# One layer with an RWKV-7 branch: the inverse's transfers on GpSimd's queue, group 1's k projected first into ar's place, and preparation and group norm in smaller pieces

## The chip, the cores and the metric

The kernel runs on one core of one Trainium2 chip. The metric is device time in microseconds of one execution, given as the median of several runs. The kernel before takes 2217.47 us (three runs, 2214.89 to 2221.9).

## The reference

The program is one layer of a streaming encoder on 256 tokens of width 2048, in fp32: a half-step SwiGLU FFN, two parallel token mixers (latent attention, MLA, and RWKV-7) with gates, a cross-attention into 256 memory tokens, and a second half-step FFN, each between two RMS norms. The change lies in the RWKV-7 mixer, which has 16 heads of width 64:

```python
p = token_shift(proj, mu_shift)              # y + (y_prev - y) * mu
r, k, v, dw, da, dg = jnp.split(p, ...)
w = -jax.nn.softplus(-(w0 + jnp.tanh(dw) @ w_w2)) - 0.5
decay = jnp.exp(-jnp.exp(w))
a = jax.nn.sigmoid(a0 + da @ w_a2)
g = jax.nn.sigmoid(dg) @ w_g2
kk = (k * k_k) per head, divided by its norm
k = k * (1.0 + (a - 1.0) * k_a)
# per token: a_in = -kk, b_in = kk * a
sa = einsum('bhvk,bhk->bhv', state, a_t)
state = state * w_t + sa * b_t + v_t * k_t   # outer products
o_t = einsum('bhvk,bhk->bhv', state, r_t)
# then, per head: o = groupnorm(o) * lnx_w + lnx_b + sum(r * k * r_k) * v
return (o * g) @ w_ob
```

## The kernel before

**Linear layers.** Every weight is loaded in tiles of 128x1024 fp32 (512 KB) by SP into one of four `wraw` buffers, then split by ScalarE (`whi`, a cast, line 319) and VectorE (`wlo`, the remainder, line 320); the halves stand in a ring of three. `lin_tok_steps` (lines 411 to 413) runs three matmuls of 512 columns for each k-step and each of two blocks of 128 tokens; `lin_ch_steps` (lines 375, 379) does the same with the weights stationary. A tile holds the weights for 2.6 us of such matmuls. `self.last_split` and `self.last_cast` name the newest split and cast emitted so far.

**Order of the work.** TensorE's order in the mixer is written by hand: `weave` runs two generators, `rwkv()` (the recurrence) and `fill()` (projections that need no recurrence). Each number that `rwkv()` yields is an amount of filling, in us as the program counts it (0.65 for one token step, 0.66 for one channel step), that goes in before `rwkv()` continues; a function that it yields means filling until that function is true. The other engines follow priorities (the recurrence behind the filling, the splits ahead of all) and the extra dependencies that `after` adds. All transfers of one engine go through that engine's queue in order: SP has the weights, GpSimd (POOL) most small transfers.

**RWKV.** The sixteen heads are two groups (g = 0, 1) of four pairs. `rw_prep` prepares one group: a low-rank matmul for decay and a (line 1038), a cumulative sum on VectorE (1057), the norm of kk (matmul ssp at 1067, a power on GpSimd at 1072, a copy to width 64 at 1077, matmul rnb at 1086), products on VectorE (lines 1088 to 1104), the bonus matmul pb (1110), and four products of 128x1024 with the exponentials, written to `bk` and `ar` (1124 to 1127). k and r of group 0 are projected ahead of the weave; those of group 1 are part of `fill()`, in slots of the tags "k" and "r", of which there is one each, so that group 0's must have been used up. `rw_gram` makes for each pair of chunks of 32 tokens the products of keys with queries, `G` (line 1159). `rw_inverse` inverts 128 triangular 32x32 blocks of it: they go from `G` to DRAM (`ld`, eight transfers), from there into a layout with one block per partition (`LT`), VectorE does 31 steps of two operations (1192, 1195), the result `TT` goes to DRAM (`td`), and `back()` brings it back into `G` in eight transfers (line 1200). Here SP issues all eighteen. `rw_chain` then goes through the eight chunks: po from values (1233) and state (1250), pu with the inverse (1261), the state's update (1277) and the output (1291). Between po of chunk 0 and its pu it yields 62.0, calls `back()` and yields 5.0; the transfers of `back()` are ordered behind the last weight load emitted. `rw_values` loads each chunk's uv on GpSimd's queue, `rw_group_norm` normalises the output of a block of 128 tokens (t = 0 in the chain, t = 1 behind it).

**v.** `rw_proj_v` projects v in two blocks; its tokens are shifted by way of DRAM (`vraw`, `vp`), and the shift's arithmetic is put off by `do_later` until k-step 8 of the next block.

## Time and profile before

| what | value |
|---|---|
| median of three runs | 2217.47 us |
| the profiled execution | 2216.08 us |
| its span (first to last instruction) | 2214.3 us |
| granted TensorE clock, mean | 0.997 |
| TensorE busy | 2181.3 us, 99% |
| VectorE busy | 1467.1 us, 66% |
| ScalarE busy | 1133.5 us, 51% |
| GpSimd busy | 93.2 us, 4% |
| from 880 to 1210 us (the weave): TensorE busy | 322.1 of 330 us |

The profile has a page of totals and several views of the trace: a table by stretches of time, groups of instructions by line, instructions in order of time (with idle time ahead of an instruction in square brackets and what ended it), and the chain of work that ended last. PE is TensorE's matmul, PEld its weight load, DVE VectorE, ACT ScalarE, POOL GpSimd and SP SyncE; a "q" behind an engine's name is its queue. L320 is line 320 of the kernel. Times in the text are microseconds from the start of the span. A matmul's recorded time overlaps the next one's, so that "busy" doesn't mean that no time is lost.

### The profile page before, as it was taken

The numbers are of one execution on the slowest core, as the hardware profiler recorded it, in microseconds if no ns is written. First come the engines' busy times: TensorE is split into PE (matmuls) and PEld (weight loads), VectorE is DVE, ScalarE is ACT, GpSimd is POOL, SyncE is SP. The second block draws the span as 40 slices with busy tenths as digits, with TensorE's granted clock in tenths as the row PEclk, the third lists the DMA queues.
The fourth block names the chain that finished last, engine by engine and source line by source line (L and its number), as shares of the span: only waits on it lengthen the run. The fifth ranks groups of instructions, "written<-read, shape, count | busy, mean of one in ns | idle before, by whom it ended". The sixth has DMA issues, their size and how long they took to land.

```text
span 2214.3 us, 35085 instructions
## 1 busy us (share of the span) xinstructions
PE 2181.3 (99%) x13664; PEld 1944.6 (88%) x13664; DVE 1467.1 (66%) x2164; ACT 1133.5 (51%) x1686; POOL 93.2 (4%) x159
## 2 busy tenths in 40 slices
PE   9999999999999999999999999999999999999997
PEld 8999999988888888888778889988999999998886
DVE  7666666654457677778678766657766666664454
ACT  7555555544446565644444556446555555554442
POOL 0000000000000100100242000000000000000000
PEclk9999999999999999999999999999999999999999
DMA  7666666666666664556767765555666666666664
GB/s 259 222 210 202 202 200 200 201 212 206 209 208 217 207 218 141 168 176 193 245 195 252 266 212 191 172 176 177 199 202 201 202 202 200 200 210 208 209 203 140
DMA packets 138567, 449.31 MB, mean 203 GB/s; under 512 B 24352, under 2 KB 25888, under 8 KB 138144
## 3 DMA queue, kind: packets, MB, share of 16 engines
q1 hardware_dynamic: 131568, 431.94, 60.4%
q0 software_dynamic: 5968, 14.69, 2.1%
q8 instruction: 107, 1.75, 0.3%
q10 hardware_dynamic: 864, 0.44, 0.1%
q14 instruction: 60, 0.49, 0.1%
HBM read 436.51 MB, written 10.49 MB: 202 GB/s over the span
## 4 chain that ended last, share of the span: by engine, by line
PE 86%; DVE 6%; DMA 3%; issue 2%; ACT 2%; POOL 1%; SPq 0%; DVEq 0%; ACTq 0%; POOLq 0%
PE mm L375 31%; PE mm L379 16%; PE mm L411 11%; PE mm L413 11%; PE mm L412 11%; DVE wlo L320 3%; ACT whi L319 1%; DVE X L621 0%; DMA uv<-vsh 0%; DVE tm L1192 0%; DVE TT L1195 0%; PE tr L515 0%; PE xo L1593 0%; DMA ab<-vsh 0%; DMA td<-TT 0%
## 5 line engine op out<-in xcount | busy, mean ns | idle before, releaser
L320 DVE TENSOR_TENSOR wlo<-wraw,whi 128x1024 fp32r<-128x1024 f32 (+3 forms) x792 | 953.5, 1206 | 611.1 <-ACT whi L319 598.9
L319 ACT CAST whi<-wraw 128x1024 fp32r<-128x1024 f32 (+3 forms) x792 | 818.1, 1034 | 789.5 <-PE mm L413 406.8
L375 PE MATMUL mm<-hT,whi 128*128 128x512 f32 x3280 | 1078.0, 383 | 0.6 <-ACT whi L319 0.5
L379 PE MATMUL mm<-hT,wlo 128*128 128x256 f32 x3280 | 881.9, 274 | 1.6 <-DVE wlo L320 1.6
L375 PEld LDWEIGHTS mm<-hT,whi 128*128 128x128 f32 x3280 | 614.4, 190 | 81.6 <-ACT whi L319 1.2
L379 PEld LDWEIGHTS mm<-hT,wlo 128*128 128x128 f32 x3280 | 630.3, 192 | 8.6 <-DVE wlo L320 2.8
L411 PE MATMUL mm<-whi,mh 128*128 128x512 f32 x680 | 257.7, 379 | 0.0
L412 PE MATMUL mm<-wlo,mh 128*128 128x512 f32 x680 | 257.7, 379 | 0.0
L413 PE MATMUL mm<-whi,ml 128*128 128x512 f32 x680 | 257.7, 379 | 0.0
L412 PE MATMUL mm<-wlo,hT 128*128 128x512 f32 (+2 forms) x512 | 180.2, 352 | 5.2 <-DVE wlo L320 5.1
L411 PE MATMUL mm<-whi,hT 128*128 128x512 f32 (+2 forms) x512 | 183.1, 358 | 1.9 <-ACT whi L319 1.7
L413 PE MATMUL mm<-whi,hT 128*128 128x512 f32 (+2 forms) x512 | 179.1, 350 | 0.3 <-DVE hT L506 0.3
L413 PEld LDWEIGHTS mm<-whi,ml 128*128 128x128 f32 x680 | 128.5, 189 | 18.2
L412 PEld LDWEIGHTS mm<-wlo,mh 128*128 128x128 f32 x680 | 128.5, 189 | 18.2
L411 PEld LDWEIGHTS mm<-whi,mh 128*128 128x128 f32 x680 | 128.5, 189 | 18.2
L387 ACT COPY half<-mm 128x256 f32<-128x256 f32 x206 | 75.6, 368 | 120.4 <-PE mm L375 120.4
L412 PEld LDWEIGHTS mm<-wlo,hT 128*128 128x128 f32 x512 | 97.5, 191 | 18.5 <-DVE wlo L320 9.4
L388 DVE TENSOR_TENSOR half<-half,mm 128x256 f32<-128x256 f32 x206 | 86.0, 418 | 40.9 <-ACT half L387 40.9
L411 PEld LDWEIGHTS mm<-whi,hT 128*128 128x128 f32 x512 | 97.5, 190 | 13.8 <-ACT whi L319 2.1
L413 PEld LDWEIGHTS mm<-whi,hT 128*128 128x128 f32 x512 | 97.4, 190 | 10.1 <-DVE hT L506 0.9
L470 POOL TENSOR_TENSOR rstd<-rstd,mhalf 128x1 f32<-128x1 f32 x22 | 14.4, 666 | 1698.2 <-DVE rstd L468 1698.2
L411 PE MATMUL mm<-whi,mT 128*128 128x512 f32 x128 | 48.7, 380 | 0.0
(305 smaller groups left out, 1752.0 us busy)
## 6 DMA issues: line engine op xcount, KB each, us to landing
wraw<-in_w_ffn_up SPq DMA_DIRECT2D x171, 512.0 KB, 3.7
wraw<-in_w_ffn_gate SPq DMA_DIRECT2D x170, 512.0 KB, 3.6
wraw<-in_w_ffn_down SPq DMA_DIRECT2D x168, 512.0 KB, 4.2
wraw<-in_w_in SPq DMA_DIRECT2D x124, 512.0 KB, 4.1
wraw<-in_w_o SPq DMA_DIRECT2D x32, 512.0 KB, 4.0
wraw<-in_w_ckv SPq DMA_DIRECT2D x32, 512.0 KB, 3.9
wraw<-in_w_oa SPq DMA_DIRECT2D x16, 512.0 KB, 3.6
wraw<-in_w_ob SPq DMA_DIRECT2D x16, 512.0 KB, 4.6
```

Of the source, the lines that this page charges most:

```text
L319: cast = self.last_cast = nc.scalar.copy(out=hi[:, e], in_=raw[:, e])
L320: self.last_split = nc.vector.tensor_sub(out=lo[:, e], in0=raw[:, e], in1=hi[:, e].bitcast(F32))
L375: both = lambda: nc.tensor.matmul(ps[j], hi[:, s], self.woven(x[:, k]), start=(k == 0), stop=(k == nk - 1))
L379: nc.tensor.matmul(ps[j][:, 0, :], lo[:, s], self.woven(x[:, k, 0]), start=False, stop=False)
L387: nc.scalar.copy(out=tokens, in_=low)
L388: nc.vector.tensor_add(tokens, tokens, high)
L411: nc.tensor.matmul(ps[t], part(xh, t, k), hi, start=(k == first), stop=False)
L412: nc.tensor.matmul(ps[t], part(xh, t, k), lo, start=False, stop=False)
L413: self.last_mm = nc.tensor.matmul(ps[t], part(xl, t, k), hi, start=False, stop=(k == last))
L470: nc.gpsimd.tensor_tensor(out=r, in0=r, in1=self.mhalf, op=ALU.pow)
```

## The change

Five things are changed. **The inverse's eighteen transfers** are issued by GpSimd instead of SP, the way back included, which now stands at the end of `rw_inverse`; `back`, the yield of 5.0 behind it and `last_fetch` are gone. **Group 1's k** is projected first, into the first half of `ar`'s part for group 1 (which is written only at the end of that group's preparation); then comes one block of `out_a`, then r, then the other three blocks of `out_a`. Before, two blocks of `out_a` came first, then k, r and the last two blocks. **Preparation:** kf, the factor of ta and the factor r_k on r go from VectorE to ScalarE; the remaining products on VectorE each stand behind the last split emitted so far (`behind`), with yields of 2.6 us between them, and so do the four products into `bk` and `ar`. **Group norm** for t = 1 stops once more in each half, and its square stands behind the last split; the yields behind the chain are changed to suit. **The shift of v** is put off to k-step 12 instead of 8.

```diff
@@ -308,7 +308,6 @@
                 e = slice(j * n, (j + step) * n)
                 early = feed is not None and k + j == 0
                 load = (nc.scalar if early else nc.sync).dma_start(out=raw[:, e], in_=src[:, e])
-                self.last_fetch = load
                 if parts and not early:
                     if feed is not None and k + j in (1, 2):
                         self.after(load, self.last_load)
@@ -940,12 +939,15 @@
             pass
         return self.rk
 
-    def rw_proj_rk_steps(self, pool, normed, g):
+    def rw_proj_rk_steps(self, pool, normed, g, k=None, between=()):
         h, row = normed.h, normed.row
         w_in = self.a["w_in"]
         r = pool.tile([P, GP, T], F32, tag="r", name="r")
-        k = pool.tile([P, GP, T], F32, tag="k", name="k")
+        if k is None:
+            k = pool.tile([P, GP, T], F32, tag="k", name="k")
         for dst, base, nm in ((k, 1856, "k"), (r, 832, "r")):
+            if dst is r:
+                yield from between
             for sl in range(2):
                 def ev(j, ps):
                     p = 2 * sl + j
@@ -1009,7 +1011,7 @@
                 self.later.append(shift)
 
             for k in self.lin_tok_steps(self.a["w_in"], KD, 2880 + c * 512, 512, h[:, :, 0], h[:, :, 1], ev):
-                if k == 8:
+                if k == 12:
                     self.do_later()
 
     def rw_alloc(self, pool):
@@ -1022,6 +1024,7 @@
     def rw_prep(self, pool, g, bon, ready):
         nc, a = self.nc, self.a
         p4 = lambda nm: pool.tile([P, GP, T], F32, tag="p4", name=nm, bufs=6)
+        behind = lambda ins: self.after(ins, self.last_split)
         ww = pool.tile([P, 512], F32, tag="ww", name="ww", bufs=2)
         cs = slice(g * 512, (g + 1) * 512)
         nc.gpsimd.dma_start(out=ww[:64], in_=a["w_w2"][:, cs])
@@ -1085,24 +1088,26 @@
                     with self.hot():
                         nc.tensor.matmul(
                             ps[:, j, t * P : (t + 1) * P], x[:, t, 2 * p2 + j], self.ident, start=True, stop=True)
-            nc.vector.scalar_tensor_tensor(
+            behind(nc.vector.scalar_tensor_tensor(
                 out=kk[:, 2 * p2 : 2 * p2 + 2, :], in0=kk[:, 2 * p2 : 2 * p2 + 2, :], scalar=-1.0, in1=ps,
-                op0=ALU.mult, op1=ALU.mult)
-        kf = p4("kf")
+                op0=ALU.mult, op1=ALU.mult))
+        kf, rk = p4("kf"), p4("rk")
         for p in range(GP):
             pg = g * GP + p
-            nc.vector.tensor_scalar(
-                out=kf[:, p, :], in0=ta[:, p, :], scalar1=self.col2("hka", pg), scalar2=self.col2("omhka", pg),
-                op0=ALU.mult, op1=ALU.add)
-        nc.vector.tensor_mul(k, k, kf)
-        nc.vector.tensor_scalar(out=ta, in0=ta, scalar1=1.0, scalar2=-0.5, op0=ALU.add, op1=ALU.mult)
-        nc.vector.tensor_mul(ta, ta, kk)
-        rk = p4("rk")
+            nc.scalar.activation(
+                out=kf[:, p, :], in_=ta[:, p, :], func=AF.Identity, scale=self.col2("hka", pg),
+                bias=self.col2("omhka", pg))
+        nc.scalar.activation(out=ta, in_=ta, func=AF.Copy, scale=-0.5, bias=-0.5)
         for p in range(GP):
-            nc.vector.scalar_tensor_tensor(
-                out=rk[:, p, :], in0=r[:, p, :], scalar=self.col("r_k", g * GP + p), in1=k[:, p, :],
-                op0=ALU.mult, op1=ALU.mult)
-        yield 13.0
+            nc.scalar.activation(
+                out=rk[:, p, :], in_=r[:, p, :], func=AF.Copy, scale=self.col("r_k", g * GP + p))
+        yield 2.6
+        behind(nc.vector.tensor_mul(k, k, kf))
+        yield 2.6
+        behind(nc.vector.tensor_mul(ta, ta, kk))
+        yield 2.6
+        behind(nc.vector.tensor_mul(rk, rk, k))
+        yield 5.2
         for t in range(NT):
             pb = self.pss.tile([P, HEADS_G], F32, tag="sm", name="pb")
             for p in range(GP):
@@ -1121,10 +1126,12 @@
         nc.scalar.activation(out=e2, in_=lw, func=AF.Exp, scale=-1.0)
         arv = self.ar[:, g].rearrange("q c p (x s) -> q p c x s", x=2)
         bkv = self.bk[:, g].rearrange("q c p (x s) -> q p c x s", x=2)
-        nc.vector.tensor_mul(bkv[:, :, :, g, :], v4(ta), v4(e2))
-        nc.vector.tensor_mul(bkv[:, :, :, 1 - g, :], v4(k), v4(e2))
-        nc.vector.tensor_mul(arv[:, :, :, g, :], v4(kk), e1[:, :, :, 0:CHUNK])
-        nc.vector.tensor_mul(arv[:, :, :, 1 - g, :], v4(r), e1[:, :, :, 1:])
+        for out, x, y in (
+            (bkv[:, :, :, g, :], v4(ta), v4(e2)), (bkv[:, :, :, 1 - g, :], v4(k), v4(e2)),
+            (arv[:, :, :, g, :], v4(kk), e1[:, :, :, 0:CHUNK]), (arv[:, :, :, 1 - g, :], v4(r), e1[:, :, :, 1:]),
+        ):
+            behind(nc.vector.tensor_mul(out, x, y))
+            yield 2.6
         nc.vector.tensor_copy(
             out=self.wc[:, :, g * GP : (g + 1) * GP].rearrange("q c p -> q p c"), in_=e1[:, :, :, CHUNK])
 
@@ -1182,8 +1189,8 @@
                                [:, :, self.role(0, 0, g)])
 
         for there, here in moves(ld):
-            nc.sync.dma_start(out=there, in_=here)
-        nc.sync.dma_start(out=LT, in_=ld.rearrange("q g c b s t -> (q g c b) s t"))
+            nc.gpsimd.dma_start(out=there, in_=here)
+        nc.gpsimd.dma_start(out=LT, in_=ld.rearrange("q g c b s t -> (q g c b) s t"))
         nc.vector.memset(TT, 0.0)
         nc.vector.memset(TT.rearrange("b s t -> b (s t)")[:, :: C + 1], 1.0)
         for s in range(C - 1):
@@ -1193,13 +1200,9 @@
                 tm[:, : s + 1, :n], TT[:, : s + 1, s : s + 1].broadcast_to(sh),
                 LT[:, s : s + 1, s + 1 :].broadcast_to(sh))
             nc.vector.tensor_add(TT[:, : s + 1, s + 1 :], TT[:, : s + 1, s + 1 :], tm[:, : s + 1, :n])
-        nc.sync.dma_start(out=td.rearrange("q g c b s t -> (q g c b) s t"), in_=TT)
-
-        def back():
-            for there, here in moves(td):
-                self.after(nc.sync.dma_start(out=here, in_=there), self.last_fetch)
-
-        return back
+        nc.gpsimd.dma_start(out=td.rearrange("q g c b s t -> (q g c b) s t"), in_=TT)
+        for there, here in moves(td):
+            nc.gpsimd.dma_start(out=here, in_=there)
 
     def rw_values(self, pool, c):
 
@@ -1214,7 +1217,7 @@
                     self.after(load, self.small)
         return uv
 
-    def rw_chain(self, pool, G, back):
+    def rw_chain(self, pool, G):
         nc = self.nc
         units = [(j, g, h) for j in range(GP) for g in range(2) for h in range(2)]
         block = lambda rows, c, j, g, cols: G[rows, g, c // 2, c % 2, j, cols]
@@ -1238,8 +1241,6 @@
         uvs = [self.rw_values(pool, c) for c in range(2)]
         po = from_values(0, uvs[0])
         yield 62.0
-        back()
-        yield 5.0
         for c in range(NC):
             uv = uvs[c]
             if c + 2 < NC:
@@ -1354,7 +1355,11 @@
             self.after(nc.vector.tensor_reduce(out=mean, in_=o, axis=AX.X, op=ALU.add), behind)
             nc.vector.tensor_scalar_mul(mean, mean, 1.0 / 64)
             nc.vector.tensor_sub(o, o, bc(mean))
-            nc.vector.tensor_mul(sq, o, o)
+            if t:
+                yield
+                self.after(nc.vector.tensor_mul(sq, o, o), self.last_split)
+            else:
+                nc.vector.tensor_mul(sq, o, o)
             nc.vector.tensor_reduce(out=var[-1], in_=sq, axis=AX.X, op=ALU.add)
             nc.vector.tensor_scalar(
                 out=var[-1], in0=var[-1], scalar1=1.0 / 64, scalar2=LNX_EPS, op0=ALU.mult, op1=ALU.add)
@@ -1425,10 +1430,10 @@
                         x.append(where.tile([P, 8, P], F32R, tag=tag, name="z"))
 
                 def fill():
-                    yield from self.out_a_steps(ya, range(2))
-                    yield from self.rw_proj_rk_steps(mp, normed, 1)
+                    k = self.ar[:, 1].rearrange("q c p x -> q (c p x)")[:, : GP * T].rearrange("q (p t) -> q p t", p=GP)
+                    yield from self.rw_proj_rk_steps(mp, normed, 1, k, self.out_a_steps(ya, range(1)))
                     found.add("rk")
-                    yield from self.out_a_steps(ya, range(2, 4))
+                    yield from self.out_a_steps(ya, range(1, 4))
                     found.add("ya")
                     for c in range(8):
                         s = slice(c % 4 * 512, (c % 4 + 1) * 512)
@@ -1450,7 +1455,7 @@
                     G = self.hpool.tile([P, 2, NC // 2, 2, GP, 64], F32, tag="big", name="G")
                     tc.cur_priority = base
                     yield from self.rw_gram(G)
-                    back = self.rw_inverse(pool, G)
+                    self.rw_inverse(pool, G)
                     E2, ab, scale, norm = E, {}, {}, {}
 
                     def low(f, *args):
@@ -1481,7 +1486,7 @@
                                 self.transposed(self.normed[h], zh, zl, None, 0, 4 * h)
 
                     seen = 0
-                    for want in self.rw_chain(pool, G, back):
+                    for want in self.rw_chain(pool, G):
                         if len(self.last_o) > seen:
                             seen = len(self.last_o)
                             low(behind_chunk, seen)
@@ -1491,14 +1496,14 @@
                     next(norm[1])
                     for h in range(2):
                         ab[1, h] = next(scale[1, h])
-                    for us in (10.0, 4.0, 6.5, 3.0):
+                    for us in (10.0, 2.6, 2.6, 2.6, 2.6, 2.6):
                         yield us
                         next(norm[1])
                     z_tiles(pool, "ar", "bk")
-                    yield 5.5
+                    yield 3.0
                     for h in range(2):
                         self.transposed(self.normed[h], zh, zl, None, 1, 4 * h)
-                        yield 5.0 - 3.0 * h
+                        yield 3.0 - h
 
                 self.lead = FIRST
                 self.weave(rwkv(), C, fill(), B)
```

## The prediction

> **What bounds the kernel now.** I read the shares of the page first, then the stretches' table, TensorE's order of time with the idle time ahead of each instruction, the chain of work, and last the DMA issues.
>
> ```profile
> PE 2181.3 (99%) x13664; PEld 1944.6 (88%) x13664; DVE 1467.1 (66%) x2164; ACT 1133.5 (51%) x1686; POOL 93.2 (4%) x159
> PE 86%; DVE 6%; DMA 3%; issue 2%; ACT 2%; POOL 1%; SPq 0%; DVEq 0%; ACTq 0%; POOLq 0%
> ```
>
> TensorE is the bound, in the busy shares and in the chain. The change adds and removes no matmul, so all it can return is time in which TensorE stands still or runs slow. Columns of the next fence: stretch, length, busy time of PE, PEld, DVE, ACT, POOL with instruction counts, granted clock, DMA share, GB/s.
>
> ```profile
> 740.00:760.00 20.00, 20.00 (x94) 17.53 (x93) 10.97 (x12) 11.11 (x15) 2.26 (x4) 1.00 0.63 197
> 905.00:915.00 10.00, 8.95 (x58) 7.97 (x57) 10.00 (x14) 4.81 (x6) 0.00 (x0) 1.00 0.44 152
> 1077.00:1081.00 4.00, 4.00 (x13) 3.16 (x12) 2.00 (x2) 0.94 (x2) 0.00 (x0) 0.57 0.75 227
> 1172.00:1178.00 6.00, 4.14 (x20) 3.31 (x19) 4.50 (x7) 1.48 (x2) 0.00 (x0) 1.00 0.82 243
> ```
>
> The first row is a stretch without loss: 94 matmuls of 512 columns in 20 us, about 0.215 us from start to start. One takes 0.38 us, so 0.16 us overlaps the next: idle time printed in brackets costs its figure plus 0.16. The places where TensorE waits in the change's stretch:
>
> ```profile
> 771.89 0.48 PE L412 MATMUL mm<-wlo,hT 128*128 128x512 f32 x1 [0.68 <-DVE wlo L320]
> 774.95 0.48 PE L412 MATMUL mm<-wlo,hT 128*128 128x512 f32 x1 [0.20 <-DVE wlo L320]
> 914.51 0.38 PE L379 MATMUL mm<-hT,wlo 128*128 128x256 f32 x1 [1.05 <-DVE wlo L320]
> 978.23 0.48 PE L412 MATMUL mm<-wlo,hT 128*128 128x512 f32 x1 [1.14 <-DVE wlo L320]
> 1075.34 0.48 PE L411 MATMUL mm<-whi,hT 128*128 128x512 f32 x1 [1.67 <-ACT whi L319]
> 1076.60 0.48 PE L412 MATMUL mm<-wlo,hT 128*128 128x512 f32 x1 [0.78 <-DVE wlo L320]
> 1176.93 0.48 PE L412 MATMUL mm<-wlo,hT 128*128 128x512 f32 x1 [1.86 <-DVE wlo L320]
> ```
>
> Each waits for one half of a split weight tile, and all lie next to code that the change touches.
>
> **The inverse's transfers (1075).** The chain of work there, and at the front of the inverse:
>
> ```profile
> 1006.88 4.29 DMA ld<-G
> 1011.31 4.54 DMA LT<-ld
> ...
> 1058.93 6.13 DMA td<-TT
> ...
> 1065.13 0.33 SPq L1200
> ...
> 1068.68 0.49 SPq L1200
> ...
> 1069.27 4.87 DMA wraw<-in_w_in
> 1074.24 1.05 ACT whi L319
> ```
>
> SP issues in order. It stands at the first G<-td until td has landed at 1065.06, spends 4.1 us on eight issues, and only then loads the next weight tile, which lands at 1074.14. With these on GpSimd's queue the weight loads pass. Removed: 1.67 + 0.16 = 1.83 us; the second wait, start to start, 1076.60 − 1075.34 − 0.22 = 1.04; and behind them the row 1077 to 1081, where the clock was 0.57: 4 × 0.43 = 1.7. Together **4.6 us**.
>
> Where does the stall go? The next thing to be late is the inverse itself. The five-microsecond yield behind `back()` goes too, so TensorE reaches the first pu matmul (line 1261, which reads what G<-td writes) sooner:
>
> ```profile
> 1007.66 0.69 PE L1233 MATMUL po<-uv,G 32*64 32x64 f32 x32
> 1081.50 0.65 PE L1261 MATMUL pu<-rhs,G 32*32 32x64 f32 x32
> ```
>
> At 0.65 us a step of three matmuls (really 3 × 0.2155), 62 us is 96 steps, 62.1 us; with 0.6 for po itself and about 1 for small gaps that this stretch has anyway, TensorE stands at pu at 1007.7 + 63.7 = 1071.4. Chunk 0 needs the first four of the eight G<-td: on SP the fourth is issued near 1066.6 and lands 2.3 later (row below), 1068.9. So the old queue would have left 2.5 us of slack. GpSimd's prices:
>
> ```profile
> wg<-in_w_g POOLq DMA_DIRECT2D x1, 512.0 KB, 5.4
> LT<-ld SPq DMA_DIRECT2D x1, 512.0 KB, 4.5
> td<-TT SPq DMA_DIRECT2D x1, 512.0 KB, 6.1
> osc<-o POOLq DMA_DIRECT2D x32, 32.0 KB, 4.0
> ld<-G SPq DMA_DIRECT2D x8, 64.0 KB, 3.5
> uv<-vsh POOLq DMA_DIRECT2D x32, 32.0 KB, 3.5
> G<-td SPq DMA_DIRECT2D x8, 64.0 KB, 2.3
> L1210 POOL DMA_DIRECT2D uv<-vsh x32 | 16.3, 513 | 139.1 <-DVE wlo L320 125.6 <-ACT o L1296 7.3 <-DMA t1d<-gt 2.9
> L1343 POOL DMA_DIRECT2D ov<-osc x4 | 2.2, 558 | 6.3 <-DMA osc<-o 6.2
> ```
>
> Four transfers stand in a row, each waiting for the one before: ld, LT, td, G. From issue to landing GpSimd's nearest rows are longer by 0.5 (osc against ld), 0.9 (wg against LT; the same taken for td) and 1.2 (uv against G): 3.5 us. Issue costs 0.51 us for 32 rows of 1 KB and 0.56 for 128 rows; an ld or G transfer is 32 × 16 runs of 128 bytes, 512 pieces, which the trace never shows on this queue. Extending the line, 0.045 us for 96 pieces, gives 0.74, against 0.51 on SP (3.55 us from the first to the eighth): 0.23 more, for four ld and four G issues 1.8. From above, if all 0.56 us went by the piece, 4.4 ns each, an issue takes 2.2 us and eight add 13.7. From below, if GpSimd were as quick as SP, nothing is added. I take latency in full and half the extended line's extra: 3.5 + 0.9 = 4.4, late by 4.4 − 2.5 = **1.9 us** at pu. VectorE is saturated through the inverse, so a late start isn't caught up. A wait of 1.86 us left the clock at 1.00 (row 1172 to 1178), so I add nothing for it. What stands behind the eighteen new issues on GpSimd's queue:
>
> ```profile
> 1086.72 0.56 POOL L1210 DMA_DIRECT2D uv<-vsh  x1 [122.22 <-DVE wlo L320]
> ```
>
> Chunk 3's uv, after 122 us of nothing, so they hold up nobody. Net 4.6 − 1.9 = **2.7**, bounds 4.6 and −11.8 (3.5 + 13.7 − 2.5 = 14.7 late, 1.7 of clock on top, less 4.6).
>
> The Trainium skill, "DMA: Bandwidth & Descriptors", section "Latency and other measured facts", puts the first byte at some 0.6 us on the hardware path and 1 us on GpSimd's. By that, as an estimate, four steps add 1.6 us, within the slack, and this term would be 4.6; the rows above say more than twice as much, under other load.
>
> **Preparation (914, 978).** Between 905 and 915 VectorE is busy 10.00 of 10: products of 128x1024 at 1.2 us stand two in a row ahead of a split. After, each stands behind the last emitted split, one per 2.6 us of filling (2.3 us of VectorE: one split, one product), and three operations per group go to ScalarE:
>
> ```profile
> L1094 DVE TENSOR_SCALAR kf<-ta,k 128x256 f32<-128x256 f32 x8 | 2.9, 408 | 0.0
> L1053 ACT ACTIVATE kk<-k,cols 128x256 f32<-128x256 f32 x8 | 4.2, 549 | 0.0
> ```
>
> Eight pieces of 0.55 and one of 128x1024 at about 1.1 make 5.5 us of ScalarE per group. It has 4.81 us busy in the ten shown, so they fit between casts. Gain (1.05 + 0.16) + (1.14 + 0.16) = **2.5**; bounds 2.5 and −1 (stalls stay, and a cast per group waits half a microsecond behind a piece). The longer yields, 10.4 us per group, cost nothing while there is filling: group 1's r and k are ready after 52.8 us of it (k 21.1, one out_a block 10.4, r 21.1) instead of 63, group 0's preparation then ends at 46.4, and out_a's other three blocks last to 84. The gram falls near 95 instead of 93 of 250 us.
>
> **k in ar's place, r later.** The matmuls are the same, reordered. r's first slice is evacuated at 42 us of filling, while group 0 last reads the old r at 43.8: this evacuation waits some 2 to 4 us, covered by the other two of the four PSUM tiles. Cost 0; 2 us if that cover is gone.
>
> **Value shift (771, 774)**, four k-steps later:
>
> ```profile
> 768.80 1.30 DVE L1004 TENSOR_TENSOR vp<-vp,vc 128x512 f32<-128x512 f32 x2 [3.23 <-DMA vp<-vraw]
> ```
>
> VectorE waits for the load of vp while a split stands behind it. 5.2 us later the load has landed. Gain 0.68 + 0.20 + 2 × 0.16 = **1.2**; bounds 1.2 and 0.
>
> **Group norm (1177).**
>
> ```profile
> 1173.40 0.69 DVE L1354 TENSOR_REDUCE gm<-ov 128x8 f32<-128x512 f32 x1 [2.93 <-DMA ov<-osc]
> 1175.05 0.69 DVE L1357 TENSOR_TENSOR ov<-ov 128x512 f32<-128x512 f32 x1
> 1175.66 1.22 DVE L320 TENSOR_TENSOR wlo<-wraw,whi 128x1024 fp32r<-128x1024 f32 x1
> ```
>
> Most of this wait is the transfer of ov, which isn't touched: the first yield stays at 10. Only the square (1175.05) steps behind the split: 1175.66 − 1175.05 = **0.6**, bounds 2.0 (the mean too falls behind it) and 0. The stage's yields sum to 31 us instead of 36; the filling left over is the same matmuls later.
>
> **Sum**: 2.7 + 2.5 + 0 + 1.2 + 0.6 = 7.0 us off the profiled execution's 2216.1, 2209.1. The median of the runs shown is 1.4 above that execution: **2210.5**.
>
> **Rivals.** *No new wait*: GpSimd's queue is as quick as SP's, the inverse's term is 4.6 and the time 2208.6. For it, POOL is idle there; against it, the seven landing times. *The pieces only move the stalls* (VectorE's order was full, ScalarE's new work delays casts): preparation 0, the rest as forecast, about 4 us off, 2213.5; for it, the 10.00 of 10; against it, the operations that leave VectorE. *Slower*: issuing 512 short pieces costs by the piece, up to 2.2 us an issue; pu then stands up to 14.7 us and the clock falls again. The inverse's term is −11.8 at the worst, 2.5 + 1.2 + 0.6 = 4.3 stay: 2225; it decides from about 1.3 us an issue (eight times 0.8 more, 6.4 + 3.5 − 2.5 = 7.4 late, 1.7 of clock: 9.1 against 4.6 + 4.3 = 8.9 gained). For it: no row has such pieces; against it: 0.51 and 0.56 hardly depend on the count.
> The Trainium skill, "SBUF — State Buffer", section "SBUF: two separate sides", has another road to the same place: certain VectorE operations lock GpSimd out while it writes descriptors. The trace shows GpSimd's issues holding 0.51 us on average beside a busy VectorE, so this adds little to that rival.
>
> **How the numbers follow.** Forecast 0.45, no new wait 0.18, pieces move 0.23, slower 0.14. A measurement of this kernel can tell about 0.3%, 6.6 us, from no change; the forecast's 7.0 lies just past it, so I give it 0.27 faster and 0.18 same. Faster 0.27 + 0.18 = 0.45; same 0.18 + 0.23 = 0.41; slower 0.14. The range reaches below "no new wait" by some noise, 2205.5, and up past "pieces move" into the milder part of the slower case, 2219. The likeliest case alone: 2208 to 2213.
>
> **What would show it.** Right: no wait at whi or wlo between the gram and pu, the clock 1.00 there, and a wait of 1 to 3 us at the first pu for G<-td; no waits over 1 us in preparation; the 771 pair gone; a wait near 1.2 us left behind the ov transfer. Wrong: GpSimd's ld and G issues over 1.4 us each, pu waiting over 5 us, casts on ScalarE late behind kf or rk, TensorE standing at r's evacuation, or a stall that only moved from 914 or 978 to a neighbour.

## The result, and the profile after

| | before | after |
|---|---|---|
| median | 2216.24 us (six runs, 2213.66 to 2221.9) | 2205.85 us (six runs, 2204.23 to 2207.28) |
| profiled execution, its span | 2216.08, 2214.3 us | 2206.16, 2204.0 us |
| ratio, with 95% interval | | 0.995 (0.9937 to 0.9963) |

The kernel is 10.4 us faster; 7.0 were forecast (2210.5). First the page's shares and chain, and stretches of the kernel after, with the columns of the stretches' table shown above. Every edit moves the line numbers by a few, so that `wlo`, line 320 before, is L319 in the kernel after.

```profile
PE 2177.6 (99%) x13664; PEld 1942.6 (88%) x13664; DVE 1462.3 (66%) x2148; ACT 1142.2 (52%) x1704; POOL 105.1 (5%) x177
...
PE 90%; DVE 5%; issue 2%; ACT 1%; DMA 1%; POOL 0%; SPq 0%; DVEq 0%; ACTq 0%; POOLq 0%
```

```profile
905.00:915.00 10.00, 10.00 (x57) 9.01 (x56) 10.00 (x13) 9.02 (x14) 0.00 (x0) 1.00 0.60 176
1070.00:1074.00 4.00, 4.00 (x48) 3.23 (x48) 3.45 (x5) 2.40 (x5) 0.00 (x0) 1.00 1.03 251
1077.00:1081.00 4.00, 4.00 (x76) 3.29 (x77) 2.06 (x4) 2.06 (x4) 3.41 (x7) 1.00 0.59 190
```

TensorE does the same 13664 matmuls in 3.7 us less of busy time. The stretch at 905 has lost its wait although VectorE is as full as before (10.00 of 10), and from 1077 to 1081, where the chain now runs already, the clock is 1.00 instead of 0.57. TensorE's instructions in order of time show what waits are left in the stretch that the change touches:

```profile
793.67 0.43 PE L411 MATMUL mm<-wlo,cqh 128*128 128x384 f32 x1 [0.58 <-DVE wlo L319]
801.40 0.44 PE L872 MATMUL tr<-ident,qn 128*128 128x128 f32 x2 [0.65 <-ACT qn L868]
...
1072.30 0.68 PE L1262 MATMUL pu<-rhs,G 32*32 32x64 f32 x32
...
1130.42 0.68 PE L1278 MATMUL pn<-uv,bk 64*64 64x64 f32 x28 [1.07 <-DVE uv L1268]
1142.71 1.09 PE L514 MATMUL tr<-ident,ov 128*128 128x128 f32 x8 [0.93 <-DVE S L1288]
1167.19 0.48 PE L411 MATMUL mm<-wlo,hT 128*128 128x512 f32 x1 [1.23 <-DVE wlo L319]
1181.95 0.48 PE L411 MATMUL mm<-wlo,hT 128*128 128x512 f32 x1 [0.94 <-DVE wlo L319]
```

The waits at 771, 775, 914, 978, 1075 and 1077 are gone. The first pu has no wait. Two waits are left behind the chain (1167 and 1182) where there was one. The last matmul, in TensorE's order of time, first of before and then of after:

```profile
2198.64 0.38 PE L413 MATMUL mm<-whi,ml 128*128 128x512 f32 x1
```

```profile
2193.09 0.38 PE L412 MATMUL mm<-whi,ml 128*128 128x512 f32 x1
```

TensorE gains 5.55 us; the other 4.7 lie behind its last matmul, 15.66 us to the end before and 10.94 after. The table of what SP's queue waited for from 2185 on (columns: us, times, longest) says in what, again before and then after:

```profile
SPq L1703 <- PEq L1703: 5.5, 2, 5.0
```

```profile
SPq L1708 <- PEq L1708: 0.7, 2, 0.5
```

At the kernel's end all engines meet. Before, SP was done and stood 5.0 us. The row names PE's queue; the trace's records of the sequencers show who was late: GpSimd's closing DRAIN (an instruction of its sequencer at line 1703, which isn't counted as busy), from 2202.20 to 2213.52, 11.32 us. After, it takes 4.06 us (2196.64 to 2200.70) and is over before SP is.

To compare runs stage by stage I use TensorE's **lost time**: for each matmul the time to the start of the next, less what a fifth of the matmuls of that kind stay within in all these profiles (the 20th percentile), added up between landmarks; the last column is the time from the last matmul to the end. Two further stretches, ahead of 684 us and behind the first z matmul, differ by at most 0.2 us between before and after. All in us; the rows of the runs below have the same columns behind the median of the time (where a kernel ran once, that time):

```
                       684 to first  to first  gram    chain  chain's    end
                       score (value) gram      to pu          end to z
before                     12.3       17.8     12.2    24.2    4.2      15.7
after                      12.4       15.1      7.4    24.6    5.6      10.9
```

### The profile page after: what moved, and what is told of

Same layout as the page of the kernel before. It is cut to its first block, busy times and chain, and to the rows that moved or that the text cites. A ratio compares the mean times of both kernels' runs of the same rounds, so it can differ in the third digit from the quotient of the medians.

```text
span 2204.0 us, 35077 instructions
## 1 busy us (share of the span) xinstructions
PE 2177.6 (99%) x13664; PEld 1942.6 (88%) x13664; DVE 1462.3 (66%) x2148; ACT 1142.2 (52%) x1704; POOL 105.1 (5%) x177
## 3 DMA queue, kind: packets, MB, share of 16 engines
q8 instruction: 107, 1.75, 0.3%
## 4 chain that ended last, share of the span: by engine, by line
PE 90%; DVE 5%; issue 2%; ACT 1%; DMA 1%; POOL 0%; SPq 0%; DVEq 0%; ACTq 0%; POOLq 0%
PE mm L374 32%; PE mm L378 16%; PE mm L410 13%; PE mm L412 13%; PE mm L411 12%; DVE wlo L319 2%; ACT whi L318 1%; DVE X L620 0%; PE tr L514 0%; PE xo L1598 0%; DMA wraw<-in_w_uq 0%; PE xsc L1587 0%; DMA wraw<-in_w_ffn_gate 0%; PE sc L893 0%; DMA ov<-osc 0%
## 5 line engine op out<-in xcount | busy, mean ns | idle before, releaser
L319 DVE TENSOR_TENSOR wlo<-wraw,whi 128x1024 fp32r<-128x1024 f32 (+3 forms) x792 | 953.5, 1206 | 617.6 <-ACT whi L318 606.0
```

The lines of the kernel that those rows point to most:

```text
L319: self.last_split = nc.vector.tensor_sub(out=lo[:, e], in0=raw[:, e], in1=hi[:, e].bitcast(F32))
```

## The experiments

**The kernels before and after, once more.** No edit.

> The kernel before, unchanged, profiled once more. In its first profile GpSimd's closing DRAIN ran 11.3 us and ended 9.5 us after GpSimd's last addition; in the changed kernel it ran 4.1 us, and this is 4.7 us of the difference. Theory 'program': the length follows from what the program did, so it is again 9 to 12 us and the span again near 2214. Theory 'chance': each execution draws its own length; it may come out at 4 us, and the span near 2209.5. The stalls in the weave are the same as in the first profile under both.

> The changed kernel once more, beside best2 on the same chip. Median within 1.5 us of 2205.85; profile: value stage 11.6 to 12.6 us lost, preparation 15.2, gram to pu 7.5 to 9.3, chain 24.8 to 25.6, behind it 4.4 to 5.8, end 10.9. At the first pu either no wait or up to 1.3 us for G<-td.

```
b_again  2215.27       13.1       17.8     12.6    24.3    2.1      15.7
a_again  2207.31       11.9       15.1      7.7    26.5    4.9      11.0
```

Preparation and the end repeat to 0.1 us; the DRAIN is 11.32 again and 4.05. The value stage (12.3, 13.1) and group norm (4.2, 2.1) do not, in an unchanged kernel. So a term of 1 us there can't be read from one pair of profiles, and below I compare groups. In TensorE's order of time this second execution of the kernel after has what the first had not:

```profile
1071.90 0.29 PE L1262 MATMUL pu<-rhs,G 32*32 32x64 f32 x2
1072.75 0.29 PE L1262 MATMUL pu<-rhs,G 32*32 32x64 f32 x2 [0.55 <-DMA G<-td]
1073.83 0.64 PE L1262 MATMUL pu<-rhs,G 32*32 32x64 f32 x28 [0.79 <-DMA G<-td]
```

Start to start the two waits cost 0.76 and 1.00, 1.8 us: the wait that the prediction put there (1.9). They fall into the chain's column, which is why it reads 26.5.

**The inverse's transfers alone, and their way back.** `b_pool` is before with this edit alone, `a_sp` is after with it undone:

```diff
-            nc.sync.dma_start(out=there, in_=here)
+            nc.gpsimd.dma_start(out=there, in_=here)
...
         yield 62.0
-        back()
-        yield 5.0
```

> The kernel before with only the inverse's eighteen transfers moved to GpSimd's queue and the yield of 5.0 gone. Forecast of the prediction: no wait at whi or wlo between 1050 and pu, clock 1.00 there, a wait of 1.9 us at the first pu, weave 2.7 us shorter. After the result: the wait at pu is absent or below 1 us and the weave is 4 to 5 us shorter, last matmul near 2194. Closing DRAIN of GpSimd: theory 'program, by GpSimd's own transfers': these eighteen shorten it to about 4 us, time near 2206.5 to 2207; theory 'program, by something else in the change' : it stays at 9 to 12 us, time near 2211.5; theory 'chance': anything between.

> The changed kernel with the inverse's transfers back on SP, issued from back() behind the yield of 62.0, with the yield of 5.0. The stalls at whi and wlo ahead of pu and the half clock behind them return: last matmul 4 to 5 us later than in the changed kernel, near 2197.5. Theory 'DRAIN by GpSimd's own transfers': it is 9 to 12 us again, time near 2215; theory 'by something else' or 'chance in the kernel before': DRAIN near 4 us, time near 2210.5.

```
b_pool   2209.88       14.3       17.8      9.6    26.7    2.4      11.0
a_sp     2213.29       12.1       15.1      9.4    25.5    3.5      15.7
```

Alone the edit takes 6.0 us off (ratio 0.9972, 0.9961 to 0.9983; the kernel before beside it has 2215.86). Undoing it gives back 7.4 (0.999, 0.9981 to 1.0), or 6.0 against the second median of the kernel after, 2207.31. 4.7 of each is the end, which leaves 1.3 to 2.7 us for the weave. In the profile of `b_pool`, one of its slower executions (2211.75), the weave gains nothing: its last matmul comes at 2199.02, before at 2198.64. Gram to pu is 2.6 us better, but the chain is 2.5 worse. pu waits, as forecast, and waits for VectorE once more later:

```profile
1076.98 1.05 PE L1254 MATMUL pu<-rhs,G 32*32 32x64 f32 x30 [0.71 <-DMA G<-td]
1132.05 0.64 PE L1254 MATMUL pu<-rhs,G 32*32 32x64 f32 x28 [1.62 <-DVE rhs L1248]
```

In `a_sp` the weight tile is late again, but less, and the clock stays at 1.00 behind it:

```profile
1073.98 0.48 PE L411 MATMUL mm<-whi,hT 128*128 128x512 f32 x1 [0.71 <-ACT whi L319]
1075.24 0.48 PE L412 MATMUL mm<-wlo,hT 128*128 128x512 f32 x1 [0.78 <-DVE wlo L320]
```

Gram and chain together lose 35.9 us on average in nine profiles with the transfers on SP (33.6 to 36.9; before and those variants that leave this stage alone) and 32.8 in four of the new kernel's kind (32.0 to 34.2), 3.1 less. That choice of four leaves out `b_pool` (36.3), `a_gnold` (34.5) and the two of `best2` below (32.2 and 32.4). Over all eight the mean is 33.3, and the edit is worth **2.6 us** there. Apart from `a_order` (36.0), whose chain starts late, these are all the profiles with the transfers on GpSimd.

**The value shift.** `a_shift8` is after with one number undone:

```diff
-                if k == 12:
+                if k == 8:
                     self.do_later()
```

> The changed kernel with the shift of v at k-step 8 as before. Theory 'the shift gives nothing': the waits at 771 and 775 return (0.7 and 0.2 us) and the new ones behind the value stage (0.7 and 0.8 us near 793 and 800) go; at 812 us and behind it TensorE stands within 0.4 us of the changed kernel, time within 0.5 us of it. Theory of the prediction: it gives 1.2 us, so everything from 812 on is 1.2 us later.

```
a_shift8 2207.64       16.9       15.1      7.7    25.0    5.7      11.0
```

The median lies 1.8 us above the first median of the kernel after (ratio 0.9964, 0.9951 to 0.9977) but 0.3 above the second, so the times alone show nothing. The profiled execution was the slowest of its five (2211.21, the others 2207.02 to 2208.14), and VectorE's order of time in it shows the wait at its worst:

```profile
770.75 0.69 DVE L1006 TENSOR_TENSOR vp<-vp,vc 128x512 f32<-128x512 f32 x1 [2.12 <-DMA vp<-vraw]
771.36 0.68 DVE L1007 TENSOR_TENSOR vp<-vp,g 128x512 f32<-128x512 f32 x1
771.96 1.22 DVE L319 TENSOR_TENSOR wlo<-wraw,whi 128x1024 fp32r<-128x1024 f32 x1
```

The load of vp lands between 768 and 771; with k = 8 the split stands behind it. Twelve profiles with 8 lose 12.3 to 16.9 in this stage, 13.6 on average, eight with 12 lose 11.4 to 12.9, 12.1: **1.5 us**, or 1.2 without `a_shift8`'s slow execution. The first pair (12.3 and 12.4) showed nothing because before happened to be at its best there.

**Preparation.** Before with ScalarE's share alone (`b_act`), before with the order alone (`b_behind`, whose yields come to 2.6 us more per group than those of after), and after with the filling's old order and k in its own place (`a_order`):

```diff
b_act:    kf, ta, rk by nc.scalar.activation; the three products in a row, yield 13.0
b_behind: kf, ta, rk on VectorE; they and the four into bk and ar behind(...), yields of 2.6 between
a_order:
-                    yield from self.rw_proj_rk_steps(mp, normed, 1, k, self.out_a_steps(ya, range(1)))
+                    yield from self.out_a_steps(ya, range(2))
+                    yield from self.rw_proj_rk_steps(mp, normed, 1)
```

> The kernel before with only the three operations of the preparation moved to ScalarE (kf, the factor of ta, the factor r_k on r); the products on VectorE keep their places and yields. From the first score matmul to the first gram matmul TensorE lost 17.8 us in six profiles of the kernel before and its variants, and 15.1 in four of the changed kernel. Theory 'the load moved off VectorE does it': the waits at 913 and 977 shrink, stage near 15.1 to 16. Theory 'the order does it' (each product behind a split): two or three products of 1.2 us still stand in a row ahead of a split, stage 17 to 17.8.

> The kernel before with only the order of the preparation's products changed: each on VectorE behind the last split, with yields of 2.6 between, all operations still on VectorE. Theory 'the order does it': both waits of 1.2 to 1.3 us go, stage 15.1 as in the changed kernel. Theory 'the load does it': VectorE has 5 us more per group, a split still comes late, stage 16 to 17.8.

> The changed kernel with the filling in its old order: two blocks of out_a, then k (in its own place) and r of group 1, then the other two. Theory of the prediction (the order costs and gives nothing): every stage within 0.5 us of the changed kernel, time within 1 us of 2205.85. Rival (the longer yields of the preparation need r and k early): group 1's preparation, the gram and the inverse start about 10 us of filling later; the filling runs out before the chain ends, the stages pu to the chain's end and behind it lose 5 to 10 us more, as they did where only the order of the products was changed (29.8 instead of 24.2 and 20.0 instead of 15.2), time near 2212.

```
b_act    2211.78       13.1       14.9     11.6    24.2    2.9      15.7
b_behind 2221.36       13.8       14.9      7.8    29.9    4.7      15.7   (and 4.8 more behind z)
a_order  2210.34       11.4       14.9      8.4    27.6    6.5      11.2
```

Either half of the edit removes both waits (17.8 to 14.9), so neither theory holds alone. Stretches of `b_act` and `b_behind`:

```profile
905.00:915.00 10.00, 10.00 (x66) 9.30 (x66) 10.00 (x11) 6.50 (x11) 0.00 (x0) 1.00 0.60 204
```

```profile
905.00:915.00 10.00, 10.00 (x68) 9.35 (x67) 10.00 (x14) 4.35 (x5) 0.00 (x0) 1.00 0.64 209
```

VectorE stays full and TensorE stands nowhere. The order has a price that the move to ScalarE hasn't: in `b_behind` the gram begins at 1000.0 us instead of 988.4 and the chain ends at 1174.6 instead of 1161.7, with one wait of 3.9 us for rhs in it, and behind the chain the waits pile up. With k and r early most of that seems to be paid for. Without it (`a_order`) the kernel after has a median 4.5 us above its first and 3.0 above its second (ratio 0.9974, 0.9962 to 0.9985, which overlaps with 0.9947 to 0.9974 of the second), and its profile loses 4.0 and 2.9 more than theirs. Its chain waits for G and for rhs, and what follows waits for VectorE's gate operation:

```profile
1080.51 1.03 PE L1262 MATMUL pu<-rhs,G 32*32 32x64 f32 x30 [0.86 <-DMA G<-td]
1147.12 0.64 PE L1262 MATMUL pu<-rhs,G 32*32 32x64 f32 x28 [0.93 <-DVE rhs L1256]
1171.67 0.48 PE L410 MATMUL mm<-whi,hT 128*128 128x512 f32 x1 [2.02 <-DVE gt L1386]
```

**Group norm.** After with the old pieces and yields:

```diff
-                    for us in (10.0, 2.6, 2.6, 2.6, 2.6, 2.6):
+                    for us in (10.0, 4.0, 6.5, 3.0):
```

> The changed kernel with group norm and the yields behind the chain as before. In the stage from the chain's end to the first z matmul TensorE lost 4.2 and 2.1 us in two profiles of the kernel before, and 5.6 and 5.8 in two with the new pieces. Theory 'the new pieces cost': it loses 2.1 to 4.2 us here and the time is 1.5 to 3.5 us shorter, near 2203.5. Theory of the prediction (the square behind the split gives 0.6): it loses 6.2, and the time is 0.6 longer. Rival: the loss follows from where the chain ends against the weights' transfers, and it stays at 5.6 with either.

```
a_gnold  2206.71       12.4       15.1      9.0    25.5    3.7      11.0
```

The stage loses 1.9 us less than in the first profile of after; the medians (2206.71 and 2205.85) can't be told apart, with pu waiting here and not there, so the expected 2203.5 didn't come. In nine profiles of before's kind the stage loses 3.2 on average (2.1 to 4.9), in five with the new pieces 4.8 (3.5 to 5.7): about **1.6 us lost**, though the ranges overlap. The first wait in the stage comes and goes with either (none to 2.8 us lost with the old pieces, 0.4 to 1.9 with the new ones), which speaks for the rival of the weights' transfers. The second, 1.1 us lost between 1180 and 1188, stands in four of the five new ones and in no old one. VectorE's order in the kernel after shows how it arises:

```profile
1179.47 0.69 DVE L1371 TENSOR_TENSOR ov<-ov,gv 128x512 f32<-128x512 f32 x1 [0.95 <-POOL gv L1366]
1180.08 0.68 DVE L1373 TENSOR_TENSOR ov<-ov,ab 128x512 f32<-128x512 f32 x1
1180.68 1.22 DVE L319 TENSOR_TENSOR wlo<-wraw,whi 128x1024 fp32r<-128x1024 f32 x1
```

The stops of 2.6 us ask for the scaled output before GpSimd's power is ready; VectorE waits 0.95 us with a split queued behind the next two products.

**The end.** Who sets GpSimd's DRAIN? Before with 18, 9 or 36 more transfers on GpSimd's queue that nobody waits for, with a small addition by which GpSimd learns early that G<-td has landed, and with the last update wholly on VectorE:

```diff
b_x18:        for i in range(18): nc.gpsimd.dma_start(out=dum[i], in_=piece)   # 512 pieces of 128 bytes
b_x18s, b_x9s, b_x36s:  the same with one row of 2 KB, 18, 9, 36 times
b_obs:        nc.gpsimd.tensor_add(out=seen, in0=part, in1=part)               # part of G, behind back()
b_lastv:
-                update(t, s, t == 1 and c == 2)
+                update(t, s)
```

> The kernel before with eighteen more transfers on GpSimd's queue, 512 pieces of 128 bytes each, from a weight in DRAM to unused DRAM, issued behind the load of LT; nobody waits for them. GpSimd's closing DRAIN was 11.32 us with the inverse on SP (three profiles) and 4.06 us with it on GpSimd (three profiles). Theory 'count': the number of transfers on GpSimd's queue sets it, so here it is 4.1 us. Theory 'waits': the eight waits on SP's transfers that stand ahead of GpSimd's last addition (G's buffer is that of y and X) set it; they are all still there, so it is 11.3 us.

> The kernel before with one small addition on GpSimd behind back(), 128x8, that reads G, so that GpSimd has waited for the eight G<-td transfers long before its last addition, which then waits for one SP transfer instead of eight, as in the changed kernel. Theory 'waits': closing DRAIN 4.1 us, span about 5 us shorter behind the last matmul (10.9 instead of 15.7). Theory 'count': 11.3 us, 15.7.

> The kernel before with the one piece of the last update that ScalarE and GpSimd share given to VectorE, so that GpSimd's last instruction is a power on 128x1 some 2 us earlier. Theory 'waits': the DRAIN is short and hidden behind SP, 10.9 us from the last matmul to the end and about 4.7 us off the time, unless the update on VectorE costs up to 1 us. Theory 'count': DRAIN about 9.5 us longer than GpSimd's last instruction, so it ends near 2211.5 and 2 us are gained.

> The kernel before with eighteen more GpSimd transfers of a single row of 2 KB each, in place of those of 512 pieces. The closing DRAIN was 11.32 us without them, 4.46 with eighteen of 512 pieces. Theory 'number of transfers': 4.5 us. Theory 'number of pieces': near 11.3 us.

> The kernel before with nine more GpSimd transfers of one row of 2 KB. It has 115 transfers on GpSimd's queue, and its closing DRAIN ends 9.5 us after GpSimd's last addition; with eighteen more, 133, 1.1 us after. Theory 'it grows with the count and falls back at a round number between' (128): at 124 transfers about 10.3 us after the addition. Theory 'more transfers, shorter': about 5 us. Theory 'a few are enough': 1 to 2 us.

> The kernel before with thirty-six more GpSimd transfers of one row, 151 in all. Theory 'it grows with the count and falls back at 128': at 23 past it some 2 to 3 us after the addition, more than the 1.1 at 133. Theory 'more transfers, shorter' or 'a few are enough': 1 us or less.

```
          transfers on     DRAIN ends after GpSimd's    last matmul    time
          GpSimd's queue   last operation               to the end
before        115                9.5 us                   15.7        2216.08
b_obs         115                9.5                      15.7        2215.91
b_lastv       115                9.5                      13.0        2213.4 (median)
b_x9s         124               10.2                      16.4        2218.37
b_x18s        133                1.1                      10.8        2212.84
b_x18         133                2.6                      10.8        2212.7
b_x36s        151                2.5                      10.8        2207.51
after         133                2.2                      10.9        2206.16
```

The time is that of the one profiled execution, except where it says median. The theory of waits falls with `b_obs`. The number of transfers sets it, and the four counts fit a sawtooth: 0.08 us more for each transfer ((10.2 − 9.5)/9 and (2.5 − 1.1)/18), and a fall of some 9 us between 124 and 133. SP's wait for the others says the same, `b_x9s` and then `b_x18s`:

```profile
SPq L1706 <- PEq L1706: 6.2, 2, 5.8
```

```profile
SPq L1706 <- PEq L1706: 0.7, 2, 0.5
```

Where exactly it falls, and what GpSimd does in that time, stays open. `b_lastv` ends GpSimd's last operation 2.6 us sooner after the last matmul and moves the DRAIN with it (ratio 0.9985, 0.9975 to 0.9996).

**What the stages speak for.** `a_lastv` is after with the last update on VectorE; `best2` is before with the transfers on GpSimd, ScalarE's share of the preparation (products in a row, yields as before), k-step 12 and the last update on VectorE, with the filling's order and group norm untouched. `best2_again` is the same kernel beside `a_again` on one chip.

> The changed kernel with the shared piece of the last update on VectorE. In the kernel before this let SP issue its last transfer of the output about 1.7 us sooner after the last matmul, and 2.6 us came off the end. Expected here: the end 9.2 us behind the last matmul instead of 10.9, GpSimd's closing DRAIN still hidden, time 2204.1 against 2205.85. Rival: the output's last transfers lie on SP's own issue of eight and their landing, and it stays at 10.9.

> The kernel before with four edits that the runs so far speak for: the inverse's transfers on GpSimd, the preparation's three operations on ScalarE (order and yields as before), the shift of v at k-step 12, the last update wholly on VectorE. Group norm and filling order as before. By the stages measured: value 12.2, preparation 14.9, gram to pu 7.3 to 9.5, chain 24.5 to 26.6, behind it 2.4 (against 4.3 to 5.7 of the changed kernel), end 9.2: time 2202 to 2204 against 2203.9 of the changed kernel with the last update on VectorE. If the products in a row cost later (chain), 2205.

> best2 once more, beside the changed kernel on the same chip. If its parts hold (end 1.7 us shorter, behind the chain 1.5 to 2.8 us less), its median is 3 to 4.5 us under that of the changed kernel; if the difference of the two earlier medians (4.0 us, taken on different calls) came from the chip, it is under 1.5 us.

```
a_lastv      2203.9    11.5       15.1      7.3    24.9    4.3       9.2
best2        2201.81   11.8       14.9      7.7    24.5    2.7       9.2
best2_again  2202.75   12.9       14.9      8.4    24.0    3.1       9.2
```

`a_lastv` cuts the end by 1.7 us in the profile; its ratio (0.9949, 0.9937 to 0.9961) isn't apart from that of after. `best2` is: 2202.75 beside 2207.31, ratios 0.9933 (0.9921 to 0.9946) and 0.9961 (0.9947 to 0.9974). The slowest of its five executions there (2203.17) is quicker than the quickest of the kernel after (2206.24). So it beats both kernels with half of the change and one edit more: of the 4.6 us between the medians 1.7 are the last update's. That order and group norm cost the rest isn't shown by the times, since `a_lastv` and the first `best2` (0.994, 0.9926 to 0.9953) can't be told apart.

## Why the prediction was right and wrong

| step | forecast | measured (groups of profiles) |
|---|---|---|
| inverse: stalls and clock less the new wait | 2.7 | 2.6 (gram and chain); 1.3 to 2.7 by the medians |
| preparation | 2.5 | 2.7 |
| k in ar's place | 0 | 0 on its own stage; without it the new yields seem to cost 3 to 4.5 |
| value shift | 1.2 | 1.2 to 1.5 |
| group norm | 0.6 | −1.1 to −1.6 |
| the end | none | 4.7 |
| sum | 7.0 | 10.4 (the medians) |

The rows on the right come from different groups of profiles and are good to about 1 us, except preparation and the end, which repeat.

**The step that failed is one that is not there.** The sum takes "7.0 us off the profiled execution's 2216.1" and leaves all behind the last matmul as it was. 4.7 us came from there, by a side effect of the very transfers that I priced one by one: eighteen more on GpSimd's queue. Without the end, 5.7 of the 10.4 us are left for the 7.0 forecast. That the time still falls inside the range, at its lower edge, is luck: that edge was drawn from the case without a new wait, not from the kernel's end. The row of SP's 5.0 us wait stood in the profile of before, among the waits of SP's queue, which the prediction doesn't read. What the DRAIN depends on could not be read from it; that SP stood 5 us at the end for another engine could.

**Group norm had the wrong sign.** In the first pair the first wait fell from 1.86 to 1.23 us, by the 0.6 forecast for the square behind the split, but that is luck: in the other profiles this wait is anything from none to 2.8 us lost. And I priced that stop alone and took the shorter yields for the same work later. They set the next operations ahead of GpSimd's power (the second wait, 1.1 us lost). For preparation the prediction named a stall that only moves to a neighbour, for group norm it didn't; its rival ("the pieces only move the stalls") fits group norm and is false of preparation.

**Inverse.** Gross 4.6, less 1.9 of a new wait: that wait was absent in the first profile after, 1.8 us in the second, 1.25 in `b_pool`. Both the forecast and the rival "no new wait" occur, because the slack is about nothing. The gross part varies too: in two of the nine profiles with the transfers on SP (`b_lastv`, `b_x36s`) the clock doesn't fall. That the net came out at 2.6 to 3.1 is in part luck, since the parts of the new wait were wrong and made up for each other. The transfers by the time from issue to landing, after:

```profile
ld<-G POOLq DMA_DIRECT2D x8, 64.0 KB, 3.3
LT<-ld POOLq DMA_DIRECT2D x1, 512.0 KB, 3.8
td<-TT POOLq DMA_DIRECT2D x1, 512.0 KB, 5.1
G<-td POOLq DMA_DIRECT2D x8, 64.0 KB, 5.9
...
L1205 POOL DMA_DIRECT2D G<-td x8 | 5.2, 656 | 5.1 <-issue 5.1
```

I took 4.0, 5.4, 7.0 and 3.5. The large ones are quicker here than they were on SP's queue (4.5 and 6.1), which also carries the weights, but not in every execution: LT took 3.7 to 5.1 us in the nine profiles with GpSimd against 3.9 to 4.7 on SP, td 4.6 to 6.3 against 4.2 to 7.3. The one of short pieces into SBUF is much slower in all of them (5.0 to 7.0 against 2.3 to 2.6). Together the four are 1.7 us longer in this pair, where 3.5 were forecast. The estimate by the Trainium skill, "DMA: Bandwidth & Descriptors", section "Latency and other measured facts" (0.4 us a step, 1.6 in all), comes near this pair's sum and has none of the four. Issue takes 0.66 us for 512 pieces, against 0.74 by the extended line and 0.51 on SP: the slower case, which began at 1.3, is refuted.

**Preparation** went as forecast, though either half would have done. ScalarE's pieces cost what their rows said. The step "The longer yields, 10.4 us per group, cost nothing while there is filling" held only for the amount of filling, not for the place of what comes behind.

**Value shift**: right, but the first pair of profiles shows zero, and only the groups show it. The waits at 793 and 801 come with either k-step.

**Small slips in the sums.** By their own terms k, r and one out_a block make 52.6 us of filling, not 52.8, and the case where the pieces only move the stalls is 4.5 us off, 2213.0, not 2213.5. VectorE, called saturated through the inverse, is busy 50.2 of the 54 us from 1008 to 1062. None of it changes the forecast.

## What to carry to other kernels

Before summing the stalls of a stage, read what lies between the last instruction of the bound engine and the end, and which engine is late there; here eighteen transfers on another queue moved it by 4.7 us. Price the operation that follows a moved one too: work in smaller pieces is only better while each piece's input is ready when it is asked for. Where two executions of an unchanged kernel differ by more than a term in its stage, that term is read from groups of profiles, and a group takes in every profile that has the edit.

## What the runs showed of the hardware

**GpSimd's closing DRAIN depends on the number of its transfers**, and the four counts seen (115, 124, 133, 151) fit a sawtooth, 0.08 us for each and a fall of 9 us between 124 and 133; eighteen of 512 pieces in place of single rows add 1.5 us (2.6 against 1.1).

**Whether a wait halves the clock depends on where it falls.** Stretches of four microseconds behind a wait, `a_sp`, `b_act`, `b_pool` and `a_shift8`:

```profile
1075.50:1079.50 4.00, 4.00 (x45) 3.27 (x48) 2.71 (x3) 2.02 (x2) 0.00 (x0) 1.00 0.72 216
```

```profile
1074.00:1078.00 4.00, 4.00 (x13) 3.20 (x12) 1.93 (x2) 0.77 (x2) 0.00 (x0) 0.58 0.82 224
```

```profile
773.50:777.50 4.00, 3.79 (x17) 3.01 (x18) 3.96 (x6) 1.04 (x1) 1.09 (x2) 1.00 0.63 222
```

```profile
773.50:777.50 4.00, 4.00 (x12) 3.26 (x13) 3.84 (x5) 0.00 (x0) 1.09 (x2) 0.60 0.67 231
```

Ahead of them TensorE lost 0.87 + 1.04 us in two waits (clock 1.00), 1.22 + 1.04 (0.58), 2.08 in one (1.00) and 2.19 in one (0.60). A clock of 0.57 to 0.60 over 4 us is half speed for 3.2 to 3.4. By these four the limit would lie near 2.2 us lost. But in `b_x9s` TensorE lost 2.8 us in one wait and the clock stayed at 1.00; the wait, and the two stretches that it lies in:

```profile
1178.47 0.48 PE L412 MATMUL mm<-wlo,hT 128*128 128x512 f32 x1 [2.63 <-DVE wlo L320]
```

```profile
1173.28:1176.69 3.41, 2.56 (x12) 1.90 (x11) 1.65 (x4) 0.84 (x1) 0.00 (x0) 1.00 0.91 304
1176.69:1180.11 3.42, 1.64 (x8) 1.45 (x9) 3.42 (x5) 0.97 (x2) 0.07 (x1) 1.00 0.43 158
```

In `a_shift8` the whole wait lies in one such stretch, and the next one runs at 0.50:

```profile
769.84:773.25 3.41, 1.38 (x8) 0.87 (x6) 2.50 (x4) 1.04 (x1) 0.00 (x0) 1.00 0.07 30
773.25:776.66 3.41, 3.41 (x8) 2.78 (x9) 3.38 (x5) 0.00 (x0) 1.09 (x2) 0.50 0.61 200
```

These stretches are not chosen freely. The clock records of all twenty profiles know only 1.0 and 0.5, and the time between two changes is always a whole multiple of 3.413 us, so each execution has a grid of windows of that length (the last record, cut off by the end of the trace, aside). Up to 2150 us, all nine windows at full clock in which TensorE stood idle for 1.98 us or more were followed by half clock, none with less than 1.75 were, and between 1.75 and 1.87 both occur. A wait that a window's edge divides can so go free where a shorter one within a window costs 1.7 us, half of 3.41. The Trainium skill, "TensorE: Matmul & The Clock Gate", section "What's actually happening", gives windows of about 3.4 us and half speed after at least one idle window: the length agrees, but here a window that was idle for little more than half of its time was enough.
